# A softmax and matmul kernel for attention: fewer instructions on VectorE and SyncE, wider tiles for them, and an aligned loop head on SyncE

## The chip, the cores and the metric

The kernel runs on one core of one Trainium2 chip. The time is that of the device for one execution, in microseconds (us). The kernel before takes 1068.48 us, the median of three runs (1068.08 to 1069.45). One further execution was recorded by the hardware profiler: 1067.78 us, of which the span from the first to the last recorded instruction is 1066.0 us.

The engines are named as the profile names them: PE (TensorE: matrix products, and transposes done as products), DVE (VectorE), ACT (ScalarE), POOL (GpSimd) and SP (SyncE), which here issues all transfers between the chip's memory and the core's own (DMA). Each engine runs a program of its own in order and waits on semaphores for the others.

## What is computed

```python
def reference(scores: np.ndarray, v: np.ndarray) -> np.ndarray:
    scores_max = np.max(scores, axis=-1, keepdims=True)
    attn = np.exp(scores - scores_max)
    attn = attn / (np.sum(attn, axis=-1, keepdims=True) + 1e-8)
    return np.matmul(attn, v).astype(np.float32)
```

`scores` is 8 x 12 x 1024 x 1024 and `v` 8 x 12 x 1024 x 64, both float32 and normally distributed: 96 heads, of which each is 1024 queries by 1024 keys.

## The kernel before

The 96 heads are taken four at a time (`AHEAD = 4`), so the loop has 24 iterations, and k (0 to 3) is the head within one. A head has eight row groups r of 128 queries (`R = 8`), and a row group has eight blocks of 128 keys (`C = 8`). The maximum is not subtracted: exp is taken directly, and a check at the end says whether that was admissible.

One row group goes through four steps:

- ACT takes exp of the scores (L414), from the 4 MB tile `s_nat` of its head to `p_nat` in float16, two row groups with one instruction (one at a time in head 3 after its first).
- PE transposes its eight blocks (L427) into a `psT` tile. There are four of these, one per row group in turn.
- DVE copies `psT` to `pt` (L434), also four tiles in turn.
- PE multiplies `pt` with `vones` (L173), which holds v and a column of ones, so that each row's sum comes out beside its result, in `psO`. These products are done three row groups behind the transposes (`LAG = 3`). PE's order is fixed by `in_line`: transposes of a row, then the products of the row three before.

Four row groups (`G = 4`) share a bank of PSUM, and each bank is a `psO` tile of its own. When a bank is full, `invert` takes the reciprocal of the four sums on DVE (L150) and `normalise` multiplies (L158, two instructions of 64 partitions) into `out_sb`. `watch_v` has DVE reduce the absolute values of a head's `vones` (L287), one instruction for each head, in heads 0 and 1; `spread_of` and `within` (L281 to L308) derive `fits` from them. POOL brings v into `vones` (`spread_v`, L270).

At the end of an iteration (`last`) the two banks of head 3 are normalised; then `spread_of(seen, ...)` and `judge` reduce all reciprocals, and a product (L324) counts the partitions that are in range; it is on PE ahead of the next iteration's first transposes. In the last iteration `end` takes the place of the first part: ACT multiplies bank 0 of the last head (L216, four instructions), DVE inverts and multiplies bank 1, and two stores write `done`. After the loop all engines load `count` (L468) and jump over `general()`, a slow general path that is not executed with these data.

SP issues the loads in the order of use. A load of head k's scores for the next iteration waits until ACT has read the tile. The last iteration's scores are loaded in pieces (4 and 4 rows, 3, then 2, 1, 1, 1), so that work can begin before all have come.

The tile framework makes one instruction wait for another by the tiles that they write and read; `rewrite`, `apart` and `after` take out or add some of these orders by hand.

Of the kernel before, what the change touches and what calls it, by code (L numbers as in the profile page):

```python
# [8 lines left out]
FP32 = mybir.dt.float32  # L9
# [17 lines left out]
def kernel(  # L27
# [68 lines left out]
    small_pool = ctx.enter_context(tc.tile_pool(name="small", bufs=1))  # L96
    seen = small_pool.tile([P, 1 + AHEAD * R + 1], FP32, name="seen")
    nc.vector.memset(seen, 1.0)
    done = small_pool.tile([P, R * D], FP32, name="done")
    v_seen = small_pool.tile([P, 1 + AHEAD + 1], FP32, name="v_seen")  # L100
    nc.vector.memset(v_seen, 1.0)
# [38 lines left out]

    def sums(k, st, b):

        psO = st["psO"][b][:, 0 : G * M].rearrange("p (g m) -> p g m", m=M)
        at = 1 + k * R + b * G
        recip = seen[:, at : at + G].rearrange("p (g o) -> p g o", o=1)
        return psO, recip

    def invert(k, st, b):
        psO, recip = sums(k, st, b)
        return nc.vector.reciprocal(out=recip, in_=psO[:, :, D : D + 1])  # L150

    def normalise(k, st, b):

        psO, recip = sums(k, st, b)
        h = k % T
        for t in range(T):
            part = slice(t * W, (t + 1) * W)
            nc.vector.tensor_tensor(  # L158
                out=st["out_sb"][h * W : (h + 1) * W, t, b * G : (b + 1) * G, :],
                in0=psO[part, :, 0:D],  # L160
                in1=recip[part].to_broadcast([W, G, D]),
                op=mybir.AluOpType.mult,
            )

    def finish(u):

        n0, k, r, pt, st = u
        b, g = r // G, r % G
        if r == 0:
            st["out_sb"] = out_bufs[k // T]  # L170
        bank = st["psO"][b]
        for c in range(C):
            product = nc.tensor.matmul(  # L173
                out=bank[:, g * M : (g + 1) * M],
                lhsT=pt[:, c * P : (c + 1) * P],
                rhs=st["vones"][:, c, 0:M],
                start=(c == 0),
                stop=(c == C - 1),
            )
# [24 lines left out]
    def end(st):  # L204
# [10 lines left out]
        for g in range(G):  # L215
            nc.scalar.mul(done[:, g * D : (g + 1) * D], psO[:, g, 0:D], recip[:, g, :])  # L216
        invert(k, st, 1)
        psO, recip = sums(k, st, 1)
        nc.vector.tensor_tensor(
            out=done[:, G * D :].rearrange("p (g d) -> p g d", d=D),  # L220
            in0=psO[:, :, 0:D],
            in1=recip.to_broadcast([P, G, D]),
            op=ALU.mult,
# [43 lines left out]
    def spread_v(k):  # L267

        for s in range(S):
            spread = nc.gpsimd.tensor_copy(  # L270
                out=vones_bufs[k][s * Q : (s + 1) * Q, :, 0:D].rearrange(
                    "i (h l) d -> i h l d", l=L
                ),
                in_=v_sb[k * Q : (k + 1) * Q, :, s],
            )
            for watch in watches:
                apart(spread, watch, "products in between")

    def spread_of(tile, n):

        nc.vector.tensor_reduce(out=tile[:, 0:1], in_=tile[:, 0 : n + 1], axis=X, op=ALU.min)  # L281
        nc.vector.tensor_reduce(  # L282
            out=tile[:, n + 1 : n + 2], in_=tile[:, 1 : n + 2], axis=X, op=ALU.max
        )

    def watch_v(k, behind):
        watch = nc.vector.tensor_reduce(  # L287
            out=v_seen[:, 1 + k : 2 + k],
            in_=vones_bufs[k][:, :, 0:D],
            axis=mybir.AxisListType.XY,  # L290
            op=ALU.max,
            apply_absolute_value=True,
        )
        after(watch, behind)
        watches.append(watch)

    def within(out, tile, n, low, high, also=None):
        part = small("part")
        if also is None:
            nc.vector.tensor_scalar(  # L300
                out=part, in0=tile[:, n + 1 : n + 2], scalar1=high, scalar2=None, op0=ALU.is_le
            )
        else:
            nc.vector.scalar_tensor_tensor(  # L304
                out=part, in0=tile[:, n + 1 : n + 2], scalar=high, in1=also,
                op0=ALU.is_le, op1=ALU.mult,
            )
        nc.vector.scalar_tensor_tensor(  # L308
            out=out, in0=tile[:, 0:1], scalar=low, in1=part, op0=ALU.is_ge, op1=ALU.mult
        )  # L310

# [4 lines left out]
    count = small_pool.tile([1, 1], I32, name="count")  # L316
    fits, right = small("fits"), small("right", FP16)

    def judge(bank):

        within(right, seen, AHEAD * R, 1.0 / SUM_MAX, 1.0, also=fits[:])
        cell = bank[0:1, G * M : G * M + 1]
        in_line(
            nc.tensor.matmul(  # L324
                out=cell, lhsT=right[:], rhs=vones_bufs[0][:, 0, D : D + 1], start=True, stop=True
            )
        )
        nc.vector.tensor_copy(out=count[:], in_=cell)  # L328

    def general():  # L330
# [7 lines left out]
        lift, den = small("lift"), small("den")  # L338
        nc.vector.memset(s_bufs[0][:, 3, 0 : C * M], 1.0)
        half = SK // 2  # L340
        with tc.For_i(0, BH * R, 1) as n:
            nc.sync.dma_start(out=row, in_=s_rows[bass.ds(n, 1)].rearrange("o p j -> (o p) j"))
# [5 lines left out]
            for c in range(C):  # L348
                at = c * P % half
                nc.tensor.transpose(  # L350
                    out=psO_bufs[c * P // half][:, at : at + P],
                    in_=p_row[:, c * P : (c + 1) * P],
                    identity=ident32[:],
                )
            for h in range(2):
                nc.vector.tensor_copy(out=pt[:, h * half : (h + 1) * half], in_=psO_bufs[h][:, 0:half])
            for c in range(C):
                nc.tensor.matmul(
                    out=psO_bufs[2][:, 0:M],
                    lhsT=pt[:, c * P : (c + 1) * P],  # L360
# [4 lines left out]
            nc.vector.tensor_scalar(  # L365
                out=den, in0=psO_bufs[2][:, D : D + 1], scalar1=EPS, scalar2=None, op0=ALU.add
            )
            nc.vector.reciprocal(out=den, in_=den)
            nc.vector.tensor_scalar(
                out=out_row, in0=psO_bufs[2][:, 0:D], scalar1=den[:], scalar2=None, op0=ALU.mult  # L370
            )
            nc.sync.dma_start(
# [32 lines left out]
    def heads(n0):  # L405

        for k in range(AHEAD):
            st = dict(vones=vones_bufs[k], psO=[take(psO_bufs) for b in range(R // G)])
            for r in range(R):
# [14 lines left out]
                p_row = p_nat[:, r % EB, :].rearrange("p (h q l) -> p h l q", q=P, l=L)  # L424
                psT = take(psT_bufs)
                for c in range(C):
# [5 lines left out]
                    in_line(turned)  # L432
                pt = take(pt_bufs)
                copy = nc.vector.tensor_copy(out=pt[:], in_=psT[:])  # L434
# [15 lines left out]
        last(n0, st)  # L450
        spread_of(seen, AHEAD * R)
        judge(st["psO"][-1])

# [47 lines left out]
```

## Time and profile before

| what | us |
|---|---|
| median of three runs | 1068.48 |
| profiled execution | 1067.78 |
| its span | 1066.0 |
| PE busy with products and transposes | 727.3 (68%) |
| DVE busy | 786.2 (74%) |
| ACT busy | 741.1 (70%) |
| POOL busy | 244.8 (23%) |
| ACT waiting for scores (L414) | 173.2 |
| last row of scores landed | 1052.05 |
| last product starts | 1055.68 |
| last stores landed | 1059.84 and 1060.49 |

The granted clock of PE over the span was 0.825 of full speed. The core moved 453 MB on its DMA queue, 433 GB/s over the span. An engine's busy share is a mean over the whole span; what counts is what each engine waits for at one place. In the lines of the profile a group of instructions has its line in the kernel, engine, operation, tiles (out<-in), shape and count, then its busy time and the mean of one in ns, then the idle time ahead of it with what ended most of that. In a timeline a line has its start, its duration, the engine, the line, and in brackets the idle time ahead of it with what ended it.

### The profile page before, as it was taken

To read this page: it belongs to the slowest core of one execution; us is meant where nothing else is said; L and a number is where in the kernel's file an instruction comes from. 1 tells how busy PE (TensorE), PEld (TensorE's weight loads), DVE (VectorE), ACT (ScalarE), POOL (GpSimd) and SP (SyncE) were. 2 spreads that over 40 slices of the span, in tenths; PEclk is the share of its full clock that TensorE was granted. 3 is DMA by queue.
4 is the path that set the end of the run, shared out by engine and by line. 5 is a ranking of instruction groups with operands and counts; after the bars stand their busy time and mean duration, and the time that the engine had idled before them with its cause. 6 is when DMAs were issued, how large, how long until landed. Compare 5 with 4: busy or idle time off the path is not lost.

```text
span 1066.0 us, 33658 instructions
## 1 busy us (share of the span) xinstructions
PE 727.3 (68%) x12312; PEld 692.9 (65%) x12312; DVE 786.2 (74%) x1660; ACT 741.1 (70%) x484; POOL 244.8 (23%) x406
## 2 busy tenths in 40 slices
PE   2766866677766667676676766767766667666775
PEld 2766756666766667666675766667765667666674
DVE  1876867868678677776777777868677677786786
ACT  3756776666867668586676776666767668586685
POOL 3113212131121311212113211131121311212113
PEclk9888888878788888887888888878788787887888
DMA  9999999999999999999999999999999999999995
GB/s 393 431 423 434 424 438 430 432 432 428 432 433 433 429 436 433 433 433 432 434 427 439 433 433 433 431 435 432 433 432 433 422 440 433 432 432 427 434 427 206
DMA packets 25014, 453.08 MB, mean 425 GB/s; under 512 B 2800, under 2 KB 2800, under 8 KB 9392
## 3 DMA queue, kind: packets, MB, share of 16 engines
q1 hardware_dynamic: 25008, 453.00, 99.1%
q8 instruction: 4, 0.07, 0.0%
q14 instruction: 2, 0.02, 0.0%
HBM read 436.21 MB, written 25.17 MB: 433 GB/s over the span
## 4 chain that ended last, share of the span: by engine, by line
DMA 61%; PE 11%; PEld 8%; ACT 5%; DVE 5%; issue 4%; POOL 2%; SPq 1%; POOLq 1%; ACTq 0%; DVEq 0%
DMA s_nat<-in_scores_dram 61%; PE psT L427 6%; ACT p_nat L414 5%; PE psO L173 5%; PEld L427 5%; DVE pt L434 5%; PEld L173 4%; POOL vones L270 2%; SPq L261 1%; SPq L249 0%; POOLq L270 0%; POOLq L385 0%; POOLq L461 0%; POOLq L389 0%; DVE out_sb L158 0%
## 5 line engine op out<-in xcount | busy, mean ns | idle before, releaser
L414 ACT ACTIVATE p_nat<-s_nat 128x2048 f16<-128x2048 f32 (+1 forms) x456 | 709.4, 1630 | 219.0 <-DMA s_nat<-in_scores_dram 173.2
L427 PE MATMUL psT<-order,p_nat 128*128 128x128 f16 x6144 | 570.3, 251 | 227.5 <-ACT p_nat L414 216.3
L434 DVE COPY pt<-psT 128x1024 f16<-128x1024 f16 x768 | 513.9, 687 | 189.1 <-PE L173 77.3
L427 PEld LDWEIGHTS <-p_nat 128*128 128x128 f16 x6144 | 461.3, 125 | 244.8 <-ACT p_nat L414 232.6
L270 POOL CAST vones<-v_sb 32x512 f16<-32x512 f32 x400 | 244.1, 610 | 814.1 <-PE L427 385.0
L173 PE MATMUL psO<-vones,pt 128*128 128x65 f16 x6144 | 358.5, 205 | 34.6 <-DVE pt L434 33.0
L173 PEld LDWEIGHTS <-pt 128*128 128x128 f16 x6144 | 301.2, 106 | 48.7 <-DVE pt L434 42.6
L158 DVE TENSOR_TENSOR out_sb<-psO,seen 64x256 f32<-64x256 f32 x380 | 160.2, 422 | 63.6 <-DMA out_dram<-out_sb 52.4
L414 ACT ACT_TABLE_LOAD x24 | 30.8, 1283 | 94.1 <-PE psO L173 52.8
L287 DVE TENSOR_REDUCE v_seen<-vones 128x1 f32<-128x512 f16 x96 | 65.1, 679 | 0.8
L324 PE MATMUL psO<-vones,right 128*1 128x1 f16 x24 | 3.9, 164 | 69.2 <-DVE right L308 69.2
L324 PEld LDWEIGHTS <-right 128*1 128x1 f16 x24 | 1.9, 79 | 72.2 <-DVE right L308 72.2
L150 DVE RECIPROCAL seen<-psO 128x4 f32<-128x4 f32 x192 | 33.7, 176 | 8.6 <-PE psO L173 8.6
L308 DVE SCALAR_TENSOR_TENSOR right<-seen,part 128x1 f16<-128x1 f32 x24 | 10.5, 437 | 0.8
L308 DVE SCALAR_TENSOR_TENSOR fits<-v_seen,part 128x1 f32<-128x1 f32 x24 | 10.0, 415 | 0.0
L328 DVE CAST count<-psO 1x1 int32<-1x1 f32 x24 | 3.5, 146 | 6.2 <-PE psO L324 6.2
L304 DVE SCALAR_TENSOR_TENSOR part<-seen,fits 128x1 f32<-128x1 f32 x24 | 4.6, 192 | 0.8
L281 DVE TENSOR_REDUCE seen<-seen 128x1 f32<-128x33 f32 x24 | 4.5, 187 | 0.8
L281 DVE TENSOR_REDUCE v_seen<-v_seen 128x1 f32<-128x5 f32 x24 | 3.8, 159 | 0.7
L282 DVE TENSOR_REDUCE seen<-seen 128x1 f32<-128x33 f32 x24 | 4.2, 177 | 0.0
L282 DVE TENSOR_REDUCE v_seen<-v_seen 128x1 f32<-128x5 f32 x24 | 3.6, 149 | 0.0
L300 DVE TENSOR_SCALAR part<-v_seen 128x1 f32<-128x1 f32 x24 | 3.5, 144 | 0.0
(12 smaller groups left out, 2.8 us busy)
## 6 DMA issues: line engine op xcount, KB each, us to landing
s_nat<-in_scores_dram SPq DMA_DIRECT2D x96, 4096.0 KB, 32.3
v_sb<-in_v_dram SPq DMA_DIRECT2D x24, 1024.0 KB, 18.5
out_dram<-out_sb SPq DMA_DIRECT2D x47, 512.0 KB, 26.2
s_nat<-in_scores_dram SPq DMA_DIRECT2D x2, 2048.0 KB, 31.3
s_nat<-in_scores_dram SPq DMA_DIRECT2D x1, 1536.0 KB, 32.2
s_nat<-in_scores_dram SPq DMA_DIRECT2D x3, 512.0 KB, 20.7
s_nat<-in_scores_dram SPq DMA_DIRECT2D x1, 1024.0 KB, 25.1
out_dram<-out_sb SPq DMA_DIRECT2D x1, 256.0 KB, 3.0
```

The costliest lines, as they stand in the source:

```text
L150: return nc.vector.reciprocal(out=recip, in_=psO[:, :, D : D + 1])
L158: nc.vector.tensor_tensor(out=st["out_sb"][h * W : (h + 1) * W, t, b * G : (b + 1) * G, :], in0=psO[part, :, 0:D], in1=recip[part].to_broa ...
L173: product = nc.tensor.matmul(out=bank[:, g * M : (g + 1) * M], lhsT=pt[:, c * P : (c + 1) * P], rhs=st["vones"][:, c, 0:M], start=(c == 0) ...
L261: nc.sync.dma_start(out=v_sb[:].rearrange("x h s l d -> x (h s l d)"), in_=rows[bass.ds(n // AHEAD, 1)].rearrange("o x y -> (o x) y"),)
L270: spread = nc.gpsimd.tensor_copy(out=vones_bufs[k][s * Q : (s + 1) * Q, :, 0:D].rearrange("i (h l) d -> i h l d", l=L), in_=v_sb[k * Q : ( ...
L281: nc.vector.tensor_reduce(out=tile[:, 0:1], in_=tile[:, 0 : n + 1], axis=X, op=ALU.min)
L282: nc.vector.tensor_reduce(out=tile[:, n + 1 : n + 2], in_=tile[:, 1 : n + 2], axis=X, op=ALU.max)
L287: watch = nc.vector.tensor_reduce(out=v_seen[:, 1 + k : 2 + k], in_=vones_bufs[k][:, :, 0:D], axis=mybir.AxisListType.XY, op=ALU.max, appl ...
L308: nc.vector.scalar_tensor_tensor(out=out, in0=tile[:, 0:1], scalar=low, in1=part, op0=ALU.is_ge, op1=ALU.mult)
L414: exp = nc.scalar.activation(out=p_nat[:, g : g + rows, :].rearrange("p r (x v) -> p x r v", v=Q * L), in_=s_bufs[k][:, r + g : r + g + ro ...
L427: turned = nc.tensor.transpose(out=psT[:, c * P : (c + 1) * P], in_=p_row[:, c // L, c % L, :], identity=order16[:],)
L434: copy = nc.vector.tensor_copy(out=pt[:], in_=psT[:])
```

## The change

VectorE's and SyncE's programs get fewer instructions, and the head of the loop is aligned to the beginning of an instruction block on SyncE alone.

- The four `vones` tiles become one with a dimension for the head, set by one memset. `watch_v` reduces all four heads at once, at row 5 of head 0, and two instructions derive `fits` (which POOL sets to 1 once ahead of the loop).
- `psT` and `pt` are two tiles of two row groups each. In heads 0 and 1 one DVE copy moves both row groups; in heads 2 and 3 each is copied by itself, as before.
- `psO` is two tiles of two banks each, one for a head. Head 0 inverts and normalises both banks at once after its last row; the other heads do it bank by bank as before.
- In `general()` some of DVE's instructions move to ACT and POOL, and its loop synchronises with registers.
- `count` is loaded without a bounds check.
- `For_i` gets `head_align_engines=[SP]`.

The transfers are the same in number, size and order.

```diff
-    vones_bufs = []
-    for k in range(AHEAD):
-        vo = const_pool.tile([P, C, D + 2], FP16, name=f"vones{k}")
-        nc.vector.memset(vo[:, :, D : D + 2], 1.0)
-        vones_bufs.append(vo)
+    vones = const_pool.tile([P, AHEAD, C, D + 2], FP16, name="vones")
+    nc.vector.memset(vones[:, :, :, D : D + 2], 1.0)
...
-    pt_bufs = buffers(sb_pool, 4, [P, SK], FP16, "pt")
+    pt_bufs = buffers(sb_pool, 2, [P, EB, SK], FP16, "pt")
...
-    psT_bufs = buffers(ps_pool, 4, [P, SK], FP16, "psT")
+    psT_bufs = buffers(ps_pool, 2, [P, EB, SK], FP16, "psT")
...
-    psO_bufs = buffers(ps_pool, 2 * (R // G), [P, 512], FP32, "psO")
+    psO_bufs = buffers(ps_pool, 2, [P, R // G, 512], FP32, "psO")
...
+    def sums(k, st, *banks):
+
+        b, n = banks[0], len(banks)
+        psO = st["psO"][:, b : b + n, 0 : G * M].rearrange("p b (g m) -> p b g m", m=M)
         at = 1 + k * R + b * G
...
-        if g == G - 1 and k < AHEAD - 1:
+        if k == 0 and r == R - 1:
+            invert(k, st, 0, 1)
+            normalise(k, st, 0, 1)
+        if 0 < k < AHEAD - 1 and g == G - 1:
             invert(k, st, b)
             normalise(k, st, b)
...
-            nc.scalar.mul(done[:, g * D : (g + 1) * D], psO[:, g, 0:D], recip[:, g, :])
+            nc.scalar.mul(done[:, g * D : (g + 1) * D], psO[:, 0, g, 0:D], recip[:, 0, g, :])
...
-    def watch_v(k, behind):
+    def watch_v(behind):
+
         watch = nc.vector.tensor_reduce(
-            out=v_seen[:, 1 + k : 2 + k],
-            in_=vones_bufs[k][:, :, 0:D],
-            axis=mybir.AxisListType.XY,
+            out=most,
+            in_=vones[:, :, :, 0:D],
+            axis=mybir.AxisListType.XYZ,
             op=ALU.max,
             apply_absolute_value=True,
         )
         after(watch, behind)
         watches.append(watch)
...
+        for bound, op in ((V_MIN, ALU.is_ge), (V_MAX, ALU.is_le)):
             nc.vector.scalar_tensor_tensor(
+                out=fits, in0=most, scalar=bound, in1=fits, op0=op, op1=ALU.mult
+            )
...
+    nc.gpsimd.memset(fits, 1.0)
...
-        with tc.For_i(0, BH * R, 1) as n:
+        with tc.For_i(0, BH * R, 1, iteration_sync="reg_based") as n:
...
-            st = dict(vones=vones_bufs[k], psO=[take(psO_bufs) for b in range(R // G)])
+            st = dict(psO=take(psO_bufs))
...
-                psT = take(psT_bufs)
+                if r % EB == 0:
+                    psT2, pt2 = take(psT_bufs), take(pt_bufs)
+                psT, pt = psT2[:, r % EB, :], pt2[:, r % EB, :]
...
-                pt = take(pt_bufs)
-                copy = nc.vector.tensor_copy(out=pt[:], in_=psT[:])
-                rewrite(pt, copy)
-                if k < AHEAD // 2 and r in (G - 1, R - 2):
-                    watch_v(2 * k + (r > G), copy)
-                if k == AHEAD // 2 and r == 1:
-                    spread_of(v_seen, AHEAD)
-                    within(fits, v_seen, AHEAD, V_MIN, V_MAX)
+                if k < 2 and r % EB == EB - 1:
+                    copy = nc.vector.tensor_copy(out=pt2[:], in_=psT2[:])
+                    rewrite(pt2, copy)
+                if k >= 2:
+                    copy = nc.vector.tensor_copy(out=pt, in_=psT)
+                    rewrite(pt2, copy)
+                if k == 0 and r == R - 3:
+                    watch_v(copy)
...
-        0, BH, AHEAD, iteration_sync="reg_based"
+        0, BH, AHEAD, iteration_sync="reg_based", head_align_engines=[mybir.EngineType.SP]
...
-    good = nc.values_load(count[:], min_val=0, max_val=P)
+    good = nc.values_load(
+        count[:], min_val=0, max_val=P,
+        skip_runtime_bounds_check_because="a count of partitions, which is compared and no address",
+    )
```

More of the change, by code (lines that the diff above doesn't have):

```diff
@@ L139, in one, with invert, normalise @@
         return bh[bass.ds(n, 1)].rearrange("o p r d -> (o p) r d")
-    def sums(k, st, b):
-        psO = st["psO"][b][:, 0 : G * M].rearrange("p (g m) -> p g m", m=M)
+    def sums(k, st, *banks):
+        b, n = banks[0], len(banks)
+        psO = st["psO"][:, b : b + n, 0 : G * M].rearrange("p b (g m) -> p b g m", m=M)
         at = 1 + k * R + b * G
-        recip = seen[:, at : at + G].rearrange("p (g o) -> p g o", o=1)
+        recip = seen[:, at : at + n * G].rearrange("p (b g o) -> p b g o", b=n, o=1)
         return psO, recip
[L148 to L155, printed above, removed]
+    def invert(k, st, *banks):
+        psO, recip = sums(k, st, *banks)
+        return nc.vector.reciprocal(out=recip, in_=psO[:, :, :, D : D + 1])
+    def normalise(k, st, *banks):
+        psO, recip = sums(k, st, *banks)
+        b, n, h = banks[0], len(banks), k % T
         for t in range(T):
@@ L158, in normalise @@
             nc.vector.tensor_tensor(
[L159 to L161 removed]
+                out=st["out_sb"][h * W : (h + 1) * W, t, b * G : (b + n) * G, :].rearrange(
+                    "x (b g) d -> x b g d", b=n
+                ),
+                in0=psO[part, :, :, 0:D],
+                in1=recip[part].to_broadcast([W, n, G, D]),
                 op=mybir.AluOpType.mult,
@@ L170, in finish @@
             st["out_sb"] = out_bufs[k // T]
-        bank = st["psO"][b]
         for c in range(C):
             product = nc.tensor.matmul(
-                out=bank[:, g * M : (g + 1) * M],
+                out=st["psO"][:, b, g * M : (g + 1) * M],
                 lhsT=pt[:, c * P : (c + 1) * P],
-                rhs=st["vones"][:, c, 0:M],
+                rhs=vones[:, k, c, 0:M],
                 start=(c == 0),
@@ L219, in end @@
         nc.vector.tensor_tensor(
-            out=done[:, G * D :].rearrange("p (g d) -> p g d", d=D),
-            in0=psO[:, :, 0:D],
-            in1=recip.to_broadcast([P, G, D]),
+            out=done[:, G * D :].rearrange("p (b g d) -> p b g d", b=1, d=D),
+            in0=psO[:, :, :, 0:D],
+            in1=recip.to_broadcast([P, 1, G, D]),
             op=ALU.mult,
@@ L295, in watch_v @@
         watches.append(watch)
[L297 to L301, printed above, removed]
-            )
[L303 to L310, printed above, removed]
+        for bound, op in ((V_MIN, ALU.is_ge), (V_MAX, ALU.is_le)):
+            nc.vector.scalar_tensor_tensor(
+                out=fits, in0=most, scalar=bound, in1=fits, op0=op, op1=ALU.mult
+            )
     def small(name, dtype=FP32):
@@ L316 @@
     count = small_pool.tile([1, 1], I32, name="count")
-    fits, right = small("fits"), small("right", FP16)
+    most, fits, right = small("most"), small("fits"), small("right", FP16)
+    nc.gpsimd.memset(fits, 1.0)
     def judge(bank):
-        within(right, seen, AHEAD * R, 1.0 / SUM_MAX, 1.0, also=fits[:])
-        cell = bank[0:1, G * M : G * M + 1]
+        n = AHEAD * R
+        part = small("part")
+        nc.vector.tensor_reduce(out=seen[:, 0:1], in_=seen[:, 0 : n + 1], axis=X, op=ALU.min)
+        nc.vector.tensor_reduce(
+            out=seen[:, n + 1 : n + 2], in_=seen[:, 1 : n + 2], axis=X, op=ALU.max
+        )
+        nc.vector.scalar_tensor_tensor(
+            out=part, in0=seen[:, n + 1 : n + 2], scalar=1.0, in1=fits, op0=ALU.is_le, op1=ALU.mult
+        )
+        nc.vector.scalar_tensor_tensor(
+            out=right, in0=seen[:, 0:1], scalar=1.0 / SUM_MAX, in1=part, op0=ALU.is_ge, op1=ALU.mult
+        )
+        cell = bank[0:1, 1, G * M : G * M + 1]
         in_line(
             nc.tensor.matmul(
-                out=cell, lhsT=right[:], rhs=vones_bufs[0][:, 0, D : D + 1], start=True, stop=True
+                out=cell, lhsT=right[:], rhs=vones[:, 0, 0, D : D + 1], start=True, stop=True
             )
@@ L450, in heads @@
         last(n0, st)
-        spread_of(seen, AHEAD * R)
-        judge(st["psO"][-1])
+        judge(st["psO"])
     assert BH % AHEAD == 0 and BH >= 2 * AHEAD and SK == Q * S * C
```

26 lines of the change are left out of this document (9 added, 17 removed).

## The prediction

> **What bounds the kernel now.** I read the page first, then the timeline of a middle iteration, of the last iteration, and of the microseconds behind it. "T k,r" is the row of eight transposes (L427) of row group r of head k, "P k,r" its eight products (L173).
>
> ```profile
> span 1066.0 us, 33658 instructions
> ...
> q1 hardware_dynamic: 25008, 453.00, 99.1%
> ...
> L414 ACT ACTIVATE p_nat<-s_nat 128x2048 f16<-128x2048 f32 (+1 forms) x456 | 709.4, 1630 | 219.0 <-DMA s_nat<-in_scores_dram 173.2
> ...
> L434 DVE COPY pt<-psT 128x1024 f16<-128x1024 f16 x768 | 513.9, 687 | 189.1 <-PE L173 77.3
> ...
> L158 DVE TENSOR_TENSOR out_sb<-psO,seen 64x256 f32<-64x256 f32 x380 | 160.2, 422 | 63.6 <-DMA out_dram<-out_sb 52.4
> ...
> L287 DVE TENSOR_REDUCE v_seen<-vones 128x1 f32<-128x512 f16 x96 | 65.1, 679 | 0.8
> ```
>
> The DMA queue is in use for 99.1% of the span, and ACT waits 173.2 us for scores. An iteration takes 43.7 us (T 0,0 at 587.57 and, ten iterations on, at 1024.40), and that is the time of its 17.8 MB of loads and 1.0 MB of stores at 433 GB/s. The change alters no transfer, so it can win or lose at the two ends, unless the engines come to need more than 43.7 us an iteration.
>
> ```profile
> 562.62 0.64 PE L427 MATMUL psT<-order,p_nat 128*128 128x128 f16 x8 [2.67 <-ACT p_nat L414]
> 563.09 0.42 PE L173 MATMUL psO<-vones,pt 128*128 128x65 f16 x8
> 563.32 0.69 DVE L434 COPY pt<-psT 128x1024 f16<-128x1024 f16 x1 [0.49 <-PE L173]
> 563.35 0.61 PE L427 MATMUL psT<-order,p_nat 128*128 128x128 f16 x8
> ...
> 574.70 1.04 PE L427 MATMUL psT<-order,p_nat 128*128 128x128 f16 x8 [4.57 <-ACT p_nat L414]
> ...
> 583.64 0.43 PE L173 MATMUL psO<-vones,pt 128*128 128x65 f16 x8 [0.53 <-DVE pt L434]
> ...
> 1024.40 3.58 PE L427 MATMUL psT<-order,p_nat 128*128 128x128 f16 x32 [0.43 <-DVE count L328]
> 1030.09 17.50 ACT L414 ACTIVATE p_nat<-s_nat 128x2048 f16<-128x2048 f32 x10 [1.08 <-PE psT L427]
> 1039.26 0.64 PE L427 MATMUL psT<-order,p_nat 128*128 128x128 f16 x8
> 1047.10 0.61 PE L427 MATMUL psT<-order,p_nat 128*128 128x128 f16 x8
> 1053.36 0.64 PE L427 MATMUL psT<-order,p_nat 128*128 128x128 f16 x8
> 1055.16 0.93 ACT L216 ACTIVATE done<-psO,seen 128x64 f32<-128x64 f32 x4 [1.86 <-PE L173]
> 1055.68 0.43 PE L173 MATMUL psO<-vones,pt 128*128 128x65 f16 x8 [0.24 <-DVE pt L434]
> 1056.88 0.18 DVE L150 RECIPROCAL seen<-psO 128x4 f32<-128x4 f32 x1 [1.26 <-PE psO L173]
> ```
>
> In the middle TensorE stands idle ahead of T 2,0 (562.62) and T 3,0 (574.70) for 2.67 and 4.57 us: slack. The pace of one row: T to P 0.45 to 0.47, P to the next T 0.26, T to its copy 0.70, the copy 0.69. In the last iteration (T 0,0 at 1024.40, T 2,0 at 1039.26, T 3,0 at 1047.10, T 3,7 at 1053.36) it keeps up with ACT, whose ten exps run without a gap to 1047.59, and with the last rows, the last landing at 1052.05. The last product starts at 1055.68, the last reciprocal at 1056.88; the last stores land at 1060.49. After the count is read (1061.2 to 1061.9) VectorE's last branch (L469) is issued at 1062.15, and its next instruction only at 1065.19; SyncE is done at 1063.18 and the rest earlier. In that hole:
>
> ```profile
> q8 instruction: 1, 0.02, 2.0%
> q14 instruction: 1, 0.01, 1.1%
> ```
>
> These two packets, in the window 1062.2 to 1065.2, are instruction fetches (16384 and 8192 bytes, at 1063.04 and 1063.17). So 3 us are a branch that has to wait for its target's code.
>
> **The end, gained.** VectorE's compiled program shrinks from 212 instructions to 163. The branch that waited goes from about position 173 to 203; afterwards nothing lies beyond 163, and the loop's own backward jumps (168 to 19) never waited. I take the wait as gone. What is late next is SyncE: its wait for the six queues' semaphores ends at 1063.18, and without the bounds check (0.32 us between 1062.29 and 1062.62) and some of the rest at about 1062.5. So the closing barrier moves from 1065.27 to about 1062.55: -2.7 us; bounds 0 (still a miss, or a new one on SyncE) and -3.0. [...]
>
> SyncE's alignment padding is ahead of the loop, is jumped over, and SyncE idles there from 16.3 to 25.5 us: 0, and if it were on the path some tenths. One memset of vones instead of four, GpSimd's memset of fits: before the first landing, 0. The general path is not executed: 0.
>
> **The loop, lost.** The same shortening puts psT, pt, psO in two-row and two-bank tiles, and the compiled program orders by tile. Read from its waits, these are new:
> - In heads 2 and 3 the transposes of each odd row wait for the copy of the even row beside it, though they write the other half. Before, a T waited only for the copy four rows back. Behind it on TensorE stand all products and the next T.
> - In heads 1 and 2 P k,4 waits for the end of the normalising of bank 0, and the copies of rows 3 and 7 now stand behind the normalising.
> - One 128x2048 reduce of v stands between two copies of head 0.
> - At the iteration's end the normalising of bank 0 waits for the last product, 0.9 us more in front of the judging.
> - In end() ACT's four multiplications wait for the last product (before: for row 3's), and the last reciprocal waits for them.
>
> Prices. A pair in heads 2 and 3: 0.70 + 0.69 + 0.06 (copy's end to PE, the least of the 89 waits for a copy) + 0.45 + 0.26 = 2.16 us, where ACT's pace is 1.83 and rows land 0.95 apart. A pair's copy, 128x2048: not in the trace; between 2 x 0.60 (spacing of copies back to back) and 2 x 0.69; 1.2, near the spacing. The reduce: from 33 elements in 0.187 and 512 in 0.679, 2.26; at most 4 x 0.679. Normalising two banks: 1.4, between 0.84 and 1.7.
>
> Now the last iteration, step by step:
> - Its start. Before, from T 3,0 to the next T 0,0: 12.87 (574.70 to 587.57). After: three pairs and 1.45 to T 3,7, 7.9, and 1.0 for two rows at the half clock as now; 1.45 to P 3,7; from there 3.93 (583.64 to 587.57) + 0.9. Sum 15.2: 2.4 later, 1026.8.
> - T 0,0 to T 2,0 (before 14.86): T 0,5 starts 4.5 after T 0,0 and its copy 0.70 behind; then VectorE's list without a gap: three pair copies 3.6, reduce 2.26, two tests and a reciprocal 0.5, both banks 1.4, two pair copies 2.4, head 1's reciprocal with its wait 0.5, normalising 0.9, then P 1,4 and T 2,0 0.3: 17.1, +2.2.
> - Head 2 (before 7.84): four pairs 8.64, and 0.8 of the two normalisings (2 x 1.1, of which 0.70 each is under the transposes): 9.4, +1.6; 8.64 to 10.8.
> - T 3,0 to T 3,7 (before 6.26): 7.9, +1.7.
> - T 3,7 to P 3,7 (before 2.32, since VectorE was behind): 1.45, -0.9.
> - P 3,7 to the reciprocal (before 1.20): + 0.93 of ACT and 0.2 of semaphores, +1.1.
>
> Together 2.4 + 2.2 + 1.6 + 1.7 - 0.9 + 1.1 = **+8.1 us**; with the low ends +5.3, with the high ones +11.
>
> Does the middle still hide it? An iteration's own cycle becomes 15.2 + 17.1 + 9.4 = 41.7 us against 43.7; before it was some 35. Hidden, with 2 us of cover; when that is gone every microsecond costs some 23.
>
> **Sum.** The profiled execution took 1067.78 (span 1066.0): 1067.78 + 8.1 - 2.7 = 1073.2. The median is 0.7 above it: **1073.9 us**.
>
> **Rivals.**
> 1. *The waits cost nothing that counts; only the end is shorter.* For it: VectorE has fewer instructions, 32.1 us busy in 44, and half the copies are merged. It decides where the pair cycle falls to 1.9 us, the pace of the last rows, and ACT's multiplications are hidden. Then 1068.48 - 2.7 = **1065.8**, faster. Against: 0.70 + 0.69 are measured and serial.
> 2. *Losses of only 2 to 4 us*, as when pair copies and the reduce go faster than their rows: about **1069**, no change.
> 3. *A fetch miss remains*, on VectorE or newly on SyncE, so the change misses its aim: **1076.6**.
> 4. *The engines become the bound.* TensorE's granted clock is 0.5 after each 3.41 us stretch in which it streamed under 0.35 of the columns of full speed (128 in 56 ns), and 1.0 after those above 0.42. A pair is 3088 columns: in 2.16 us 0.6, safe; at the half clock a pair takes 3.1 us, 0.41, on the edge. Two such stretches more per iteration cost some 3 us, 1 us above the cover: 1073.9 + 23 = **1097**. [...]
>
> **Chances.** Forecast 0.63; rival 1 0.09; rival 2 0.09; rival 3 0.12; rival 4 0.07. A measurement of this kernel tells 0.2%, 2.1 us, from no change. Faster 0.09, same 0.10, slower 0.81. Range 1069.0 to 1079.5: the forecast's low and high ends and rivals 2 and 3; rivals 1 and 4 are outside.
>
> **What would show it.** Right: T r+1 starting 1.45 behind T r for even r in heads 2 and 3; the last reciprocal near 1065 and ACT's four multiplications behind the last product; VectorE's last branch with no hole and no instruction packet near the end; periods of 43.7. Wrong: odd rows 0.7 behind even ones; a last reciprocal before 1060; a 3 us hole at the end; idle time in the DMA row between the ends.

## The result, and the profile after

| | before | after |
|---|---|---|
| median, us | 1068.48 (1067.86 to 1069.45) | 1078.64 (1078.08 to 1080.03) |
| ratio, 95% interval | | 1.0098 [1.0084, 1.0111] |
| profiled execution / its span, us | 1067.78 / 1066.0 | 1078.08 / 1076.3 |
| last row of scores landed | 1052.05 | 1054.67 |
| T 0,0 / T 2,0 / T 3,0 / T 3,7 of the last iteration | 1024.40 / 1039.26 / 1047.10 / 1053.36 | 1029.40 / 1047.12 / 1057.13 / 1065.88 |
| last product / last reciprocal | 1055.68 / 1056.88 | 1067.30 / 1069.63 |

The changed kernel is 10.2 us slower. Its page, with the span, the granted clock in 40 slices, the loads' queue, the shares of the chain of waits by engine, and the groups that the change touched:

```profile
span 1076.3 us, 32373 instructions
...
PEclk9998989899898898998999989899999898998998
...
q1 hardware_dynamic: 25008, 453.00, 98.2%
...
PEld 38%; issue 29%; PE 18%; DVE 10%; PEldq 1%; ACT 1%; DVEq 0%; ACTq 0%
...
L405 ACT ACTIVATE p_nat<-s_nat 128x2048 f16<-128x2048 f32 (+1 forms) x456 | 709.4, 1630 | 219.6 <-PE psT L420 78.0
L420 PE MATMUL psT<-order,p_nat 128*128 128x128 f16 x6144 | 509.9, 234 | 179.4 <-DVE pt L430 146.8
...
L430 DVE COPY pt<-psT 128x1024 f16<-128x1024 f16 x384 | 264.0, 691 | 132.1 <-PE L168 83.6
L427 DVE COPY pt<-psT 128x2048 f16<-128x2048 f16 x192 | 232.0, 1221 | 103.9 <-PE L420 84.3
...
L279 DVE TENSOR_REDUCE most<-vones 128x1 f32<-128x2048 f16 x24 | 54.6, 2275 | 0.0
```

The transfers are the same bytes in the same 25008 packets, and no chain of waits leads through them any more: there is no DMA share in it. ACT, which waited most for scores, now waits most for TensorE (it waits for a free `p_nat`), and TensorE's transposes (now L420; products L168) wait 146.8 us for the one-row copies L430. VectorE is less busy (746.5 us against 786.2): it is not work that was added, but order.

The last iteration on TensorE, in order of time:

```profile
1029.40 3.39 PE L420 MATMUL psT<-order,p_nat 128*128 128x128 f16 x32 [0.43 <-DVE count L321]
...
1039.38 0.43 PE L168 MATMUL psO<-vones,pt 128*128 128x65 f16 x8 [1.74 <-DVE fits L289]
...
1044.03 0.43 PE L168 MATMUL psO<-vones,pt 128*128 128x65 f16 x8 [1.67 <-DVE pt L427]
...
1046.87 0.42 PE L168 MATMUL psO<-vones,pt 128*128 128x65 f16 x8 [1.25 <-DVE out_sb L152]
1047.12 0.61 PE L420 MATMUL psT<-order,p_nat 128*128 128x128 f16 x8
...
1048.74 0.61 PE L420 MATMUL psT<-order,p_nat 128*128 128x128 f16 x8 [0.76 <-DVE pt L430]
1049.19 0.42 PE L168 MATMUL psO<-vones,pt 128*128 128x65 f16 x8
1049.44 0.61 PE L420 MATMUL psT<-order,p_nat 128*128 128x128 f16 x8
...
1051.12 0.61 PE L420 MATMUL psT<-order,p_nat 128*128 128x128 f16 x8 [0.81 <-DVE pt L430]
```

The three products that wait 1.25 to 1.74 us are P 0,6, whose pair's copy stands behind the reduce of v (the copy ends at 1039.32; the view names the test on `fits` that runs beside its end), P 1,2, whose pair's copy stands behind the normalising of both banks of head 0, and P 1,4, which waits for the normalising of the other bank of its own tile. The last four lines are T 2,1, P 1,6, T 2,2 and T 2,3. An odd row starts 1.62 to 1.68 us behind the even row beside it, and holds up everything behind it on TensorE by 0.76 to 0.81; an even row follows after 0.70. The end, on all engines:

```profile
1067.30 0.30 PEld L168 LDWEIGHTS <-pt 128*128 128x128 f16 x8 [0.17 <-DVE pt L430]
...
1068.61 0.93 ACT L214 ACTIVATE done<-psO,seen 128x64 f32<-128x64 f32 x4 [12.68 <-PE psO L168]
1069.63 0.18 DVE L144 RECIPROCAL seen<-psO 128x4 f32<-128x4 f32 x1 [2.38 <-ACT done L214]
```

ACT's four multiplications wait for the last product, and the last reciprocal for them. VectorE's last branch is issued at 1074.74 and its next instruction follows at 1074.96; no instruction packet moves from 1074.6 to 1075.3. The 3 us hole is gone.

### The profile page after: what moved, and what is told of

Its sections match the earlier page's. It is cut to its first block, busy times and chain, and to the rows that moved or that the text cites. A ratio compares the mean times of both kernels' runs of the same rounds, so it can differ in the third digit from the quotient of the medians.

```text
span 1076.3 us, 32373 instructions
## 1 busy us (share of the span) xinstructions
PE 664.2 (62%) x12312; PEld 623.3 (58%) x12312; DVE 746.5 (69%) x1272; ACT 741.1 (69%) x484; POOL 243.4 (23%) x407
## 3 DMA queue, kind: packets, MB, share of 16 engines
q1 hardware_dynamic: 25008, 453.00, 98.2%
## 4 chain that ended last, share of the span: by engine, by line
PEld 38%; issue 29%; PE 18%; DVE 10%; PEldq 1%; ACT 1%; DVEq 0%; ACTq 0%
PEld L420 24%; PEld L168 13%; PE psT L420 12%; PE psO L168 6%; DVE pt L427 6%; DVE pt L430 2%; ACT p_nat L405 1%; DVE out_sb L152 1%; PEldq L453 0%; DVE fits L289 0%; DVE part L309 0%; PEldq L376 0%; PEldq L380 0%; DVE right L312 0%; DVE seen L144 0%
## 5 line engine op out<-in xcount | busy, mean ns | idle before, releaser
L420 PE MATMUL psT<-order,p_nat 128*128 128x128 f16 x6144 | 509.9, 234 | 179.4 <-DVE pt L430 146.8
L420 PEld LDWEIGHTS <-p_nat 128*128 128x128 f16 x6144 | 431.2, 119 | 196.9 <-issue 170.4
L168 PE MATMUL psO<-vones,pt 128*128 128x65 f16 x6144 | 323.6, 197 | 138.1 <-DVE out_sb L152 51.0
L168 PEld LDWEIGHTS <-pt 128*128 128x128 f16 x6144 | 268.9, 100 | 158.4 <-DVE pt L427 96.1
L430 DVE COPY pt<-psT 128x1024 f16<-128x1024 f16 x384 | 264.0, 691 | 132.1 <-PE L168 83.6
L427 DVE COPY pt<-psT 128x2048 f16<-128x2048 f16 x192 | 232.0, 1221 | 103.9 <-PE L420 84.3
L152 DVE TENSOR_TENSOR out_sb<-psO,seen 64x256 f32<-64x256 f32 (+1 forms) x332 | 152.9, 461 | 49.8 <-PE psO L168 28.3
L279 DVE TENSOR_REDUCE most<-vones 128x1 f32<-128x2048 f16 x24 | 54.6, 2275 | 0.0
L144 DVE RECIPROCAL seen<-psO 128x4 f32<-128x4 f32 (+1 forms) x168 | 30.5, 181 | 29.5 <-PE psT L420 14.8
L289 DVE SCALAR_TENSOR_TENSOR fits<-most,fits 128x1 f32<-128x1 f32 x48 | 7.1, 148 | 0.0
```

The source lines that it names most:

```text
L144: return nc.vector.reciprocal(out=recip, in_=psO[:, :, :, D : D + 1])
L152: nc.vector.tensor_tensor(out=st["out_sb"][h * W : (h + 1) * W, t, b * G : (b + n) * G, :].rearrange("x (b g) d -> x b g d", b=n), in0=psO ...
L168: product = nc.tensor.matmul(out=st["psO"][:, b, g * M : (g + 1) * M], lhsT=pt[:, c * P : (c + 1) * P], rhs=vones[:, k, c, 0:M], start=(c ...
L279: watch = nc.vector.tensor_reduce(out=most, in_=vones[:, :, :, 0:D], axis=mybir.AxisListType.XYZ, op=ALU.max, apply_absolute_value=True,)
L289: nc.vector.scalar_tensor_tensor(out=fits, in0=most, scalar=bound, in1=fits, op0=op, op1=ALU.mult)
L420: turned = nc.tensor.transpose(out=psT[:, c * P : (c + 1) * P], in_=p_row[:, c // L, c % L, :], identity=order16[:],)
```

## The experiments

Each is the changed kernel, or the kernel before, with the edits that the table names. All ratios are to the kernel before on the same chip; its median was 1067.97 us on the chip of e1 to e4, 1068.5 on that of e5 to e8 and 1068.55 on that of e9 to e11, so a median of one chip is not set against one of another without its ratio.

| run | psT, pt | psO | SyncE's head aligned | median, us | ratio, 95% |
|---|---|---|---|---|---|
| changed kernel | pairs | two banks | yes | 1078.64 | 1.0098 [1.0084, 1.0111] |
| e1_rows | rows | two banks | yes | 1074.03 | 1.0059 [1.0045, 1.0073] |
| e2_banks | pairs | one bank | yes | 1077.0 | 1.0083 [1.0070, 1.0097] |
| e3_both | rows | one bank | yes | 1067.9 | 0.9995 [0.9986, 1.0004] |
| e6_after_unaligned | pairs | two banks | no | 1076.56 | 1.0077 [1.0063, 1.0090] |
| e10_rows_unaligned | rows | two banks | no | 1073.11 | 1.0042 [1.0028, 1.0056] |
| e11_banks_unaligned | pairs | one bank | no | 1074.84 | 1.0058 [1.0044, 1.0072] |
| e5_both_unaligned | rows | one bank | no | 1065.77 | 0.9977 [0.9968, 0.9986] |
| e9_pair_copies | pairs, copied as pairs in all heads | two banks | no | 1072.88 | 1.0039 [1.0025, 1.0053] |
| e4_align | kernel before | | yes | 1069.27 | 1.0013 [1.0004, 1.0022] |
| e8_end | kernel before, edits of the end alone | | no | 1068.47 | 1.0000 [0.9991, 1.0009] |
| e7_before_again | kernel before, profiled once more | | no | 1069.18 (one) | |

### The tiles undone, one kind at a time

e1_rows, with one copy per row in all heads:

```diff
-    pt_bufs = buffers(sb_pool, 2, [P, EB, SK], FP16, "pt")
+    pt_bufs = buffers(sb_pool, 4, [P, SK], FP16, "pt")
...
-    psT_bufs = buffers(ps_pool, 2, [P, EB, SK], FP16, "psT")
+    psT_bufs = buffers(ps_pool, 4, [P, SK], FP16, "psT")
...
-                if k < 2 and r % EB == EB - 1:
-                    copy = nc.vector.tensor_copy(out=pt2[:], in_=psT2[:])
-                    rewrite(pt2, copy)
-                if k >= 2:
-                    copy = nc.vector.tensor_copy(out=pt, in_=psT)
-                    rewrite(pt2, copy)
+                copy = nc.vector.tensor_copy(out=pt[:], in_=psT[:])
+                rewrite(pt, copy)
```

> The changed kernel with four one-row psT and pt tiles and a copy for each row, as before; the shared psO tile of two banks, the one reduce of v and the shorter end stay. Theory (the odd row's transposes waiting for the even row's copy is the largest cost): the pair waits of heads 2 and 3 go (2.2 + 2.5 - 0.9 us of the last iteration by the two traces, and some 1.5 of its later start), so 1071 to 1073.5 us, and T to T of one pair falls to 1.4 to 1.9 us. Rival (the bank tile shared by two banks is the largest cost): 1076 or more. The four multiplications of ACT still start behind the last product in both.

e2_banks, with each bank of head 0 normalised by itself again:

```diff
-    psO_bufs = buffers(ps_pool, 2, [P, R // G, 512], FP32, "psO")
+    psO_bufs = buffers(ps_pool, 2 * (R // G), [P, 1, 512], FP32, "psO")
...
-        if k == 0 and r == R - 1:
-            invert(k, st, 0, 1)
-            normalise(k, st, 0, 1)
-        if 0 < k < AHEAD - 1 and g == G - 1:
+        if k < AHEAD - 1 and g == G - 1:
...
```

> The changed kernel with psO as four one-bank tiles again, and head 0 inverted and normalised bank by bank; the pair tiles of psT and pt, the one reduce and the shorter end stay. Theory: ACT's four multiplications start behind row 3 again (1.1 us), the turn between iterations loses 0.9 us, the products of row 4 lose their wait (0.4 to 1.5 us): 1074.5 to 1076.5 us, and the pair in heads 2 and 3 stays at 2.2 to 2.4 us. Rival (banks are the largest cost): 1072 or less.

e3_both has both edits.

> The changed kernel with both: one-row psT and pt tiles and one-bank psO tiles; the one vones tile, its one reduce, the instructions moved off VectorE in the general path, the missing bounds check and SyncE's aligned head stay. Theory: the loop is that of before in all that bounds it, and the end has no fetch wait: 1065.5 to 1067.5 us, below the kernel before; last row landed about 1052. Rival (the longer reduce of v between two copies, or the one vones tile, costs too): 1068.5 to 1071. Rival (the fetch wait comes back because VectorE's program is longer again than the changed one's): 1068 to 1069, with a hole of 3 us behind its last branch.

Rows alone give back 4.2 us, banks alone 1.6, both together 11.0 (by the differences of the ratios). The two waits lie under one another: with one gone, the other comes to the front. All three times are 0.4 to 0.5 us above the range that the theory gave: it took SyncE's aligned head, which all three keep, for nothing. TensorE in the last iteration of e1_rows, where nothing waits for a copy any more:

```profile
1043.70 0.60 PE L168 MATMUL psO<-vones,pt 128*128 128x65 f16 x8 [3.59 <-DVE out_sb L152]
1044.11 1.04 PE L418 MATMUL psT<-order,p_nat 128*128 128x128 f16 x8
...
1053.89 0.60 PE L168 MATMUL psO<-vones,pt 128*128 128x65 f16 x8 [3.02 <-DVE out_sb L152]
1054.30 1.04 PE L418 MATMUL psT<-order,p_nat 128*128 128x128 f16 x8
```

P 1,4 and P 2,4 write one bank of a tile while the other is read, and wait 3.59 and 3.02 us for the normalising, which stands behind four copies on VectorE. The granted clock is 0.53 and 0.54 in the 3.3 and 3.4 us behind these waits, and the first two rows of transposes take 1.04 us there instead of 0.61. The same kernel in two stretches behind these waits; the columns are the stretch, its length, busy time and number of instructions of TensorE's matmuls and weight loads, VectorE, ACT and GpSimd, then granted clock, DMA share and GB/s:

```profile
1043.70:1047.00 3.30, 3.30 (x45) 3.30 (x45) 1.21 (x2) 3.30 (x3) 1.12 (x2) 0.53 0.99 411
1053.90:1057.30 3.40, 3.40 (x47) 3.40 (x47) 1.32 (x2) 0.61 (x1) 0.00 (x0) 0.54 0.38 154
```

e3_both has no hole at its end either, yet comes out at the time of the kernel before, not below it: the last row lands at 1053.29, 1.2 us later than before, and from the last reciprocal to the end it takes 6.71 us. Something else costs.

### The alignment of SyncE's loop head

```diff
-        0, BH, AHEAD, iteration_sync="reg_based", head_align_engines=[mybir.EngineType.SP]
+        0, BH, AHEAD, iteration_sync="reg_based"
```

e4_align adds this argument to the kernel before, alone; e5, e6, e10 and e11 are e3, the changed kernel, e1 and e2 without it.

> The kernel before, with SyncE's aligned loop head alone. Theory: no effect, 1068.5 us within 1 us, and VectorE still waits 3 us behind its last branch. Rival (the alignment itself removes or brings a fetch wait at the end or in the loop): 1066 or less, or 1071 or more.

> The kernel with one-row and one-bank tiles (as e3_both), without SyncE's aligned loop head. Theory A (the last row landed 1.2 to 3.4 us later than in the profile of before in all five kernels that have the aligned head; the alignment slows the stream of loads): the last row lands at 1052.0 to 1052.3 and the time falls by 1.2 us against e3_both, to about 1066.5. Theory B (the landing differs from one execution to the next, whatever the kernel): 1067.9 within 0.7, and a landing anywhere between 1052 and 1055.

> The changed kernel without SyncE's aligned loop head. Theory A: 1076.0 to 1077.5 us, a landing of the last row at 1052 to 1052.5. Theory B: 1078.6 within 0.8, a landing anywhere between 1052 and 1055. In both VectorE has no hole behind its last branch; a hole on SyncE there would show what the alignment is good for.

> One-row psT and pt tiles, the shared bank tile kept (as e1_rows), without SyncE's aligned head. Theory (the aligned head costs some 2 us in any of these kernels, 1.2 of them here by the later landing): 1072.0 us within 0.8, the landing of the last row below 1052.8 and no steady drift of the landings. Rival (the aligned head costs only where the loop is as in e3_both or in the changed kernel): 1073.5 to 1074.5.

> One-bank psO tiles, the pair tiles kept (as e2_banks), without SyncE's aligned head. Theory: 1077.0 less 2 to 3.5 us (the drift of the landings was the largest here, 3.4 us), 1073.5 to 1075, and the pace of a pair in heads 2 and 3 stays at 2.2 to 2.4 us. Rival: 1076.5 to 1077.5, when the pair's wait and not the landing set that time.

> The kernel before, unchanged, profiled once more. Theory A: the last row lands at 1052.05 within 0.3 again. Theory B: it lands elsewhere, up to 1055, and the time follows it.

By the ratios the alignment costs 2.2 us in the changed kernel, 1.9 with both tiles undone, 2.7 with the banks undone, 1.8 with the rows undone and 1.4 in the kernel before, where no effect was expected. Each of the first four is a difference of two ratios and uncertain by 1.4 to 2.1 us, but all have the same sign, and the interval of e4_align lies above 1. e10_rows_unaligned came out 0.3 us above its expected range. Most of the cost is where no engine shows it: the rows of scores land later and later. How much later than in the first profile of before T 3,0 starts (computed from the traces, us; the last of the 24 iterations is left out, since there the kernels' own waits decide), and when the last row landed:

```
iteration                  2     7    12    17    23   last row landed
changed kernel           0.6   0.5   1.7   2.1   3.0   1054.67
  without alignment      0.5   0.5   0.5   0.5   0.9   1052.53
e1_rows                  0.5   0.7   1.1   1.4   1.7   1053.24
  without alignment      0.6   0.6   0.6   0.7   0.5   1052.03
e2_banks                -0.1   0.6   1.4   2.2   3.2   1055.48
  without alignment     -0.1  -0.1  -0.1  -0.1   0.7   1052.94
before, aligned (e4)    -0.1   0.3   0.7   1.1   1.5   1053.83
e3_both                 -0.1  -0.1   0.3   0.6   1.0   1053.29
  without alignment      0.1   0.1   0.1   0.1   0.6   1052.70
```

With the aligned head it grows by 0.05 to 0.16 us an iteration on average from the 2nd to the 23rd in every kernel, without it it stays flat from the 2nd to the 17th. In e7_before_again it is flat at 0.3, and the last row lands at 1052.32. The traces of e1 to e4, all with the aligned head, come from one chip and those of e5 to e11, none with it, from two others, so the drift alone could belong to a chip. Against that stands e4_align, which is slower than the kernel before on that same chip, where the kernel before has its lowest median. The bytes moved by a given time are the same before and after, up to 450 MB at 1045.4 and 1045.5 us. But from the third load on the 128 packets of one v load end within 4.73 us all through before, and within 4.77 growing to 7.35 in the changed kernel: some packets of one load come later and later than the others. In e4_align the same spread grows from 4.55 to 6.33, and ACT waits 178.1 us for scores against 173.2 in before; in e7_before_again the spread stays at 5.0. How an aligned head does that was not found. Aligned kernels also have two more instruction packets of 8192 bytes, at 22 and 27 us, and SyncE waits 0.5 us behind its last branch (in the changed kernel from 1074.65, with no instruction packet in that time), which makes the last reciprocal to the end 6.7 us instead of 6.35.

### The end alone

e8_end takes into the kernel before what the change does outside the loop: the general path's edits, and the count loaded without a bounds check.

```diff
...
-        with tc.For_i(0, BH * R, 1) as n:
+        with tc.For_i(0, BH * R, 1, iteration_sync="reg_based") as n:
...
-    good = nc.values_load(count[:], min_val=0, max_val=P)
+    good = nc.values_load(
+        count[:], min_val=0, max_val=P,
+        skip_runtime_bounds_check_because="a count of partitions, which is compared and no address",
+    )
```

> The kernel before with the edits behind the loop alone: three operations of the general path moved off VectorE, its loop synchronised by registers, count loaded without the bounds check. The loop is that of before, unaligned. Theory (VectorE's last branch waits for code because its target lies in another fetched piece; a shorter general path brings it nearer, but VectorE's loop is as long as before): with the wait gone 1065.5 to 1066.5 us; with the wait still there 1067.7 to 1068.5 us and a hole of 3 us behind the branch. I hold the first for 0.6.

A miss for the likelier expectation: the time is the same to 0.1%. VectorE still stands for 2.80 us behind its last branch (1062.80), and in that stretch, 1062.3 to 1065.4, the same two instruction packets are fetched:

```profile
q8 instruction: 1, 0.02, 2.4%
q14 instruction: 1, 0.01, 1.0%
```

The branch's target lies at about instruction 207 of VectorE's compiled program in before, 198 in e8_end, 180 in e3_both and e5_both_unaligned, 159 in the changed kernel; the first two wait, the others don't. So by these programs the loop itself had to become shorter, and one tile and one reduce of v do that without the pairs and the double bank. e5_both_unaligned keeps just these, and is the best version: 2.5 us faster than before by its ratio. Its page shows the chain through the transfers again, as before:

```profile
span 1065.2 us, 33333 instructions
...
q1 hardware_dynamic: 25008, 453.00, 99.2%
...
DMA 58%; PE 14%; PEld 5%; DVE 5%; ACT 4%; issue 4%; POOL 2%; SPq 1%; POOLq 1%; ACTq 0%; DVEq 0%
```

### A cheaper wait in the same tiles

e9_pair_copies keeps all tiles of the change, unaligned, and moves a pair in one copy in heads 2 and 3 too, so that no odd row waits for the even row's copy.

```diff
-                if k < 2 and r % EB == EB - 1:
+                if r % EB == EB - 1:
                     copy = nc.vector.tensor_copy(out=pt2[:], in_=psT2[:])
                     rewrite(pt2, copy)
-                if k >= 2:
-                    copy = nc.vector.tensor_copy(out=pt, in_=psT)
-                    rewrite(pt2, copy)
```

> The changed kernel without SyncE's aligned head, and with one copy for both rows of a pair in heads 2 and 3 too; all tiles as in the changed kernel. The odd row's transposes then have no copy of the even row to wait for. Theory (that wait sets the pace of heads 2 and 3): T to T of a pair falls from 2.4 us to 1.5 to 1.9, and the time from 1076.6 to 1071 to 1073; what stays are the waits for the bank tile. Rival (the bank tile's waits hold heads 2 and 3, the pair's wait only lies under them): 1075 to 1077.

It gives back 3.7 us of e6_after_unaligned by medians. TensorE in head 2 of the last iteration:

```profile
1044.61 0.42 PE L168 MATMUL psO<-vones,pt 128*128 128x65 f16 x8 [1.25 <-DVE out_sb L152]
1044.87 0.61 PE L420 MATMUL psT<-order,p_nat 128*128 128x128 f16 x8
...
1050.55 0.43 PE L168 MATMUL psO<-vones,pt 128*128 128x65 f16 x8 [0.91 <-DVE pt L427]
...
1053.31 0.41 PE L168 MATMUL psO<-vones,pt 128*128 128x65 f16 x8 [1.19 <-DVE out_sb L152]
```

No transpose waits for VectorE there. What is left are products that wait for a pair's copy and for the other bank; head 2 (T 2,0 to T 3,0) is 8.70 us, against 10.01 in e6_after_unaligned and 6.98 in e5_both_unaligned.

## Why the prediction was right, and where not

**Direction, mechanism and the end were right; the loss was sized too small.** The runs split the 10.2 us along the prediction's own terms, by medians:

| term | predicted | measured | by |
|---|---|---|---|
| end: the hole behind VectorE's last branch | -2.7 | -2.7 | before (1068.5) to e5_both_unaligned (1065.77) |
| the added waits | +8.1 | +10.8 | e5_both_unaligned to e6_after_unaligned |
| alignment of SyncE's head | 0 | +2.1 | e6_after_unaligned to the changed kernel |

They sum to +10.2, the whole of the result, as they must, since each starts where the one before ends. The first is seen in the profiles too: from the last reciprocal to the end it takes 9.08 us before and 6.35 in e5_both_unaligned. The point was 4.7 low, 2.7 by the waits and 2.1 by the alignment. That the range held the time is in part luck: with the end's gain come true, the waits' own upper bound, +11, gives 1076.8, and e6_after_unaligned lies inside that. The 2.1 us of the alignment, which the sum has at 0, fell into room that the range left for an end that gains nothing.

**The waits, step by step** (last iteration, changed kernel against before; predicted in brackets): T 0,0 5.0 later (2.4): T 3,0 of the iteration before starts 3.0 later, of which 2.0 go with the aligned head by e6_after_unaligned, and from there to T 0,0 it is 14.95 us (before 12.90; predicted 15.2, which against the 12.87 that it read is 2.3); T 0,0 to T 2,0 +2.9 (+2.2); head 2 +2.2 (+1.6); T 3,0 to T 3,7 +2.5 (+1.7); T 3,7 to P 3,7 -0.9 (-0.9); to the reciprocal +1.1 (+1.1, in which the 0.2 of semaphores stood as an estimate; beside ACT's 0.93 the two traces leave 0.20); from there to the end -2.4 (-2.7). The copy of a pair and the reduce of v took 1.22 and 2.28 us (1.2 and 2.26).

**The step that was mis-sized is the price of a pair in heads 2 and 3**, 0.70 + 0.69 + 0.06 + 0.45 + 0.26 = 2.16 us; it measured 2.38 (T 2,1 at 1048.74 to T 2,3 at 1051.12). The prediction took 0.70 from a transpose row to its copy. VectorE in those microseconds:

```profile
1049.41 0.69 DVE L430 COPY pt<-psT 128x1024 f16<-128x1024 f16 x1 [0.73 <-PE L168]
1050.38 0.69 DVE L430 COPY pt<-psT 128x1024 f16<-128x1024 f16 x1 [0.27 <-PE psO L168]
```

T 2,2 starts at 1049.44, and its copy at 1050.38, 0.94 later. VectorE is done with the odd row's copy at 1050.11 and T 2,2 itself has ended at 1050.05, so neither explains the start. The semaphore events in the trace of the changed kernel do. Each transpose, each product and each of their weight loads adds one to TensorE's semaphore (12312 matrix instructions, as many weight loads, 24629 events), and in this trace the events lie 0.030 us apart at the least (23185 of the 24628 steps between them are just that). A row of transposes with the products of another makes 32 events, 0.96 us of them, but TensorE is through with it in 0.70, so the events fall behind the work. Counted in the program's order, the last event of T 2,1 comes at 1049.39, 0.04 behind its end, and that of T 2,2 at 1050.35, 32 events and 0.96 later, 0.30 behind its end. The copy starts 0.02 behind that event, as do all 320 copies of this trace ahead of which VectorE is idle for more than 0.04.

So the prediction's 0.70 was read from rows ahead of which TensorE had been idle, and whose events were not behind (in the trace of before T 2,0 at 562.62, its copy at 563.32). T 2,1 right after it shows the delay there already: it ends at 563.96, its last event comes at 564.26 and its copy starts at 564.28. The 0.22 more per pair make up to 1.8 us in eight pairs. The rest of the loss in front of T 2,0 is that the reciprocal of head 0's two banks waits for P 0,7, with VectorE idle for 0.48 us, which the list "without a gap" left out. It is the same delay: P 0,7 ends at 1040.51, its last event comes at 1040.98, and the reciprocal starts at 1041.07.

**"Hidden, with 2 us of cover" was wrong, though it decided nothing.** Predicted were 15.2 + 17.1 + 9.4 = 41.7 us of an iteration's own cycle. A middle iteration of the changed kernel:

```profile
985.57 3.57 PE L420 MATMUL psT<-order,p_nat 128*128 128x128 f16 x32 [0.44 <-DVE count L321]
...
1003.82 0.41 PE L168 MATMUL psO<-vones,pt 128*128 128x65 f16 x8 [1.26 <-DVE out_sb L152]
...
1014.20 0.41 PE L168 MATMUL psO<-vones,pt 128*128 128x65 f16 x8 [0.77 <-DVE out_sb L152]
```

T 2,0 and T 3,0 follow these two products by 0.25, at 1004.07 and 1014.46, and wait for VectorE where before they waited 2.67 and 4.57 us for ACT. The iteration before this one took 43.17 us (from 942.40), this one 43.83 (to 1029.40), with two of its transpose rows behind the first four still at the lower clock (1.04 and 0.99 us, from 989.40 and 990.69; the granted clock is 0.50 up to 991.49). So the cover is 0.5 us or nothing. Rival 4's two thresholds are counted from the trace of before: there the clock was 0.5 behind each of the 102 stretches of 3.41 us that streamed under 0.35 of the columns of full speed, 1.0 behind each of the 185 above 0.42, and behind the 18 between them 0.5 eight times and 1.0 ten times. Its danger was real, but not at its place, the pairs, where the granted clock is 1.00 from 1047.12 to 1065.88 (its 0.41 at the half clock is also a slip: 3088 columns in 3.1 us are 0.44 at its own 128 columns in 56 ns). Without alignment the period stays 43.7 on average (e6_after_unaligned is 2.0 us behind before in its second T 0,0 and 2.1 in its 23rd), so the engines had not become the bound.

**"SyncE's alignment padding ... 0" was wrong.** It looked at the instructions that are jumped over, and not at what else an aligned head may do; what that is stays open. The trace of before could not show it, and no row showed the bound given, some tenths, either; the runs put 1.4 to 2.7 us in its place. Rival 3 named a new miss on SyncE at the end; there it is 0.35 us, not 2.7, and without a packet.

**The end was right in its size and half right in its reason.** That the branch waits for its target's code is read from the packets: two instruction packets move while VectorE stands for 3.04 us in before and for 2.80 in e8_end, and in the changed kernel, where it goes on 0.22 us behind its last branch, none moves from 1074.6 to 1075.3. By the target's place the wait is there at about 207 and 198 and gone at 180 and 159. e8_end shows that a shorter program is not enough by itself; that the last target must come to lie below some position between 198 and 180 is the reading that fits these programs, and no run moved the target alone.

## What to carry to other kernels

When buffers are merged into one tile, an instruction can come to wait for one that touches another part of the tile, and a wait that the steady state hides can come out at the last iteration, where no transfer covers it (in e6_after_unaligned the period stays at 43.7 us, and the time is 10.8 longer than without the waits): merge where one instruction reads or writes the whole tile, and nowhere else. Two waits that lie under one another must be undone together to be seen: here 3.5 and 1.7 us singly, 10.8 both (without the aligned head, by medians). Price an edit that no row shows, such as an alignment, by running it alone.

## What the runs showed that was not expected

- With an aligned loop head on SyncE, in the five kernels that have it, T 3,0 starts 0.05 to 0.16 us later per iteration on average and the last row of scores lands 1.2 to 3.4 us later than in the first profile of before, though the bytes moved by a given time are the same in sum (before and changed kernel): in the changed kernel the packets of one v load drift apart, from 4.77 to 7.35 us. The mechanism is open.
- In the trace of the changed kernel the events of TensorE's semaphore lie 0.030 us apart at the least (23185 of 24628 steps), and every transpose, product and weight load adds one. A row of transposes with the products of another makes 0.96 us of events in 0.70 us of work, and an engine that waits for them started up to 0.3 us later in a pair than the end of the transposes tells (1050.05 and 1050.38). A price read behind an idle TensorE misses this. No run here has fewer events, so what that would save is not shown.
- The wait of 2.8 to 3.0 us behind VectorE's last branch, with two instruction packets in it, is there with the target at position 198 and gone at 180, all or nothing in the programs here.
